# Three value-projection weight chunks loaded ahead of the second halves of x, and six row tiles in flight

## The chip, the cores and the metric

The kernel runs on one core of one Trainium2 chip. The metric is the device time of one execution in microseconds (us), given as the median of several runs of the same program. All work is in 32-bit floating point.

## What is computed

One layer of a decoder trunk over 1024 positions of width 1024: an RMS norm of `x`, one wide input projection, three branches (a spatial gate, a convolution, a cross-attention into 256 memory tokens), a gated merge, an output projection, a residual and a last norm. The change touches the start: the memory's keys and values, and the second 1024 columns of the input projection (`v`).

```python
h = rms_norm(x, norm_g[l])
z = jnp.einsum('bsd,de->bse', h, w_in[l])
v = layer_norm(jax.nn.gelu(z[..., OFF_A_V:OFF_A_V + W]), gmlp_ln_g[l], gmlp_ln_b[l])
...
mem_n = rms_norm(mem, mem_norm_g[l])
kv = jnp.einsum('bmd,de->bme', mem_n, w_kv)
...
proj = jnp.einsum('bsnw,nwd->bsnd', branches, w_branch[l])
merged = jnp.einsum('bsnd,bsnd->bsd', gates, proj)
x = x + jnp.einsum('bsd,de->bse', merged, w_out[l])
```

## The kernel before

**Products.** Every operand of a matmul is split into a high and a low part of a reduced-precision type: ScalarE casts the high part (L74), VectorE subtracts it from the source to get the low part (L75), and TensorE adds three products, high by high, low by high and high by low. A weight chunk is a tile of 128 partitions by 1024 elements (512 KB), loaded as `raw` (or `kraw`, `kvraw`) by SyncE and split into `whi` and `wlo`. The pool `raw` has three buffers, and the pool of `whi` and `wlo` has six, so three chunks of each are alive at once.

**Stages at the start.** First come the memory's keys (loop at L259, eight chunks `kraw`), then the memory's values (loop at L335, eight chunks `kvraw`, index `i` from 0 to 7), then the value projection of `x` (loop at L386). Its first pass (`th` = 0) covers the first 512 positions and takes eight weight chunks from `in_wv`, four for each half of the columns (`ch`). A chunk is 24 matmuls of 128x128 by 128x512 (L399). After the third chunk four more matmuls (L130) spread the row norms of `x` over all partitions into the tile `rb`. The second pass (`th` = 1) takes the same eight chunks for the other 512 positions. All later stages begin after that, at L445.

**Who loads what.** SyncE issues nearly all loads at the start, in the order of the program, from one queue. `xr` are the eight tiles of `x` turned round (128 channels by 1024 positions): their first halves (512 positions, 256 KB each) come during the keys and feed the first pass as `xg`; their second halves are issued at L360, all eight, at the end of the values' last chunk (`i` = 7). `xtok` are the eight row tiles of `x` (128 positions by 1024 channels, 512 KB each), used only for the sums of squares of the row norms (L135 to L138, on ScalarE for even and VectorE for odd tiles). `xt_load` loads one; `NXT` = 5 of them are started in chunks `i` = 2 to 6, and each call of `squares` that uses one up starts another, `NXT` further on. The first value-projection chunk is loaded where its loop comes to it:

```python
            if 2 <= i < 2 + NXT:
                xt_load(i - 2)
            if i in (5, 6):
                squares(1)
            if i == 7:
                for k in range(KT):
                    sload(xr[k][:, H:], xt[k][:, H:])
...
                hi, lo = wchunk(None, raw_load(wv[ch * 4 + c], True))
```

**What sets the order.** A scheduler orders the instructions of ScalarE, VectorE and TensorE; loads issued through `sload` or with `raw_load(..., True)` keep the program's order on SyncE. Each of SyncE's loads carries one of eight semaphores in turn and waits until the load eight places ahead of it has landed, so up to eight loads are in flight. GpSimd issues stores from a second queue, among them four of the keys (`kd`) and four of the values (`vd`, 512 KB each), after the values' results were taken out of PSUM (L365 on ScalarE, L366 on VectorE).

Of the kernel before, what the change touches and what calls it, by code (L numbers as in the profile page):

```python
# [19 lines left out]
KT = D // P  # L20
TT = S // P
H = 512
# [17 lines left out]
def trunk(ctx, tc, xt, x, memt, wf, wv, wkf, wkv, mem, wbr, wb1, wo, wst, bs, cols, fng, out):  # L40
# [13 lines left out]
    def nm(s):  # L54
        uid[0] += 1
        return f"{s}_{uid[0]}"

    def slot(dt=F32, shape=(P, 1024), s="s"):
        return slots.tile(list(shape), dt, tag="slot", name=nm(s))

    def op(shape=(P, 2, H), s="op"):
        return wpool.tile(list(shape), F32R, tag="op", name=nm(s), bufs=NOP)
# [4 lines left out]
    def bank(s="b"):  # L67
        return bank1.tile([P, H], F32, tag="b", name=nm(s))

    def f(ap):  # L70
        return ap.bitcast(F32)

    def split(src, hi, lo):
        A.copy(hi, src)  # L74
        V.tensor_tensor(lo, src, f(hi), ALU.subtract)  # L75

    def keep(ins):
        tc.keep_in_program_order(ins)

    def raw_load(src, pin=False):  # L80
        raw = wpool.tile([P, 1024], F32, tag="raw", name=nm("raw"), bufs=NRAW)
        ins = nc.sync.dma_start(out=raw, in_=src)
        if pin:
            keep(ins)
        return raw

    def wchunk(src, raw=None):
        hi, lo = op((P, 1024), "whi"), op((P, 1024), "wlo")
        split(raw_load(src) if raw is None else raw, hi, lo)
        return hi, lo  # L90
# [43 lines left out]
    def square(src, dst, vector=False):  # L134
        if vector:  # L135
            V.scalar_tensor_tensor(out=src, in0=src, scalar=1.0, in1=src, op0=ALU.mult, op1=ALU.mult, accum_out=dst)
        else:
            A.activation(out=src, in_=src, func=AF.Square, accum_out=dst)  # L138
# [9 lines left out]
    def store(dst, src):  # L148
        G.dma_start(out=dst, in_=src)
# [25 lines left out]
    xr = [None] * KT  # L175

    def sload(dst, src):
        keep(nc.sync.dma_start(out=dst, in_=src))
# [52 lines left out]
    def k_out(e, ps):  # L231
        hd, e2 = divmod(e, 2)
        if e2 == 0:
            kks[hd] = slot(F32R, (P, 2, 2, M), "k")
        kk = kks[hd]
        tmp = half("kt")
        V.tensor_tensor(tmp[:, :M], ps[:, :M], mrb, ALU.mult)
        split(tmp[:, :M], kk[:, 0, e2, :], kk[:, 1, e2, :])
        if e2 == 1:
            store(kdram[hd], f(kks.pop(hd)))  # L240
# [4 lines left out]
    def x_gain(k):  # L245
        v = xr[k][:, :H]
        xg[k] = slot(F32R, (P, 2, H), "xg")
        A.activation(out=xg[k][:, 0, :], in_=v, func=AF.Copy, scale=c1(COL_NORM, k))
        V.scalar_tensor_tensor(out=xg[k][:, 1, :], in0=v, scalar=c1(COL_NORM, k), in1=f(xg[k][:, 0, :]),
                               op0=ALU.mult, op1=ALU.subtract)  # L250
# [3 lines left out]
    def v_load(i):  # L254
        if i < KT:
            vraw[i] = slot(s="kvraw")
            sload(vraw[i], wkv[i])

    for g in range(2):  # L259
        pst = [bank() for _ in range(4)]  # L260
        for j in range(4):
            i = 4 * g + j
            if i == 0:
                hi, lo = op((P, 1024), "whi"), op((P, 1024), "wlo")
# [4 lines left out]
            elif g:  # L269
                hi, lo = wchunk(None, kraw[i])  # L270
            else:
                hi, lo = op((P, 1024), "whi"), op((P, 1024), "wlo")
# [4 lines left out]
            for kk2 in range(2):  # L277
                k = 2 * j + kk2
# [45 lines left out]
    def xt_load(t):  # L324
        xtok[t] = slot(s="xtok")
        sload(xtok[t], x[t * P:(t + 1) * P, :])

    def squares(n):
        for _ in range(n):
            t = min(xtok)  # L330
            square(xtok.pop(t), xss[:, t:t + 1], t % 2)
            if t + NXT < TT:
                xt_load(t + NXT)

    for hf in range(2):  # L335
        pst = [bank() for _ in range(MT)]
        for c in range(4):
            i = hf * 4 + c
            hi, lo = wchunk(None, vraw[i])
            v_load(i + 3)  # L340
            if i < 4:
                x_gain(4 + i)
            for m in range(MT):
                ms = slice(m * P, (m + 1) * P)
                for kk2 in range(2):
                    k = 2 * c + kk2
                    ws = slice(kk2 * H, (kk2 + 1) * H)
                    for j, (a, w) in enumerate(((mhi, hi), (mlo, hi), (mhi, lo))):
                        T.matmul(pst[m], a[k][:, ms], w[:, ws], start=(k == 0 and j == 0),
                                 stop=(k == KT - 1 and j == 2))  # L350
            if i < 2:
                for _ in range(2):
                    k_out(*late.pop(0))
            if 2 <= i < 2 + NXT:
                xt_load(i - 2)
            if i in (5, 6):
                squares(1)
            if i == 7:
                for k in range(KT):
                    sload(xr[k][:, H:], xt[k][:, H:])  # L360
        vv = [slot(F32R, (P, 2, MT, HD), "v") for _ in range(2)]
        for m in range(MT):
            for hh in range(2):
                hs = slice(hh * HD, (hh + 1) * HD)
                A.activation(out=vv[hh][:, 0, m, :], in_=pst[m][:, hs], func=AF.Copy, scale=mr[:, m:m + 1])  # L365
                V.scalar_tensor_tensor(out=vv[hh][:, 1, m, :], in0=pst[m][:, hs], scalar=mr[:, m:m + 1],  # L366
                                       in1=f(vv[hh][:, 0, m, :]), op0=ALU.mult, op1=ALU.subtract)
        for hh in range(2):
            store(vdram[hf * 2 + hh], f(vv[hh]))
# [16 lines left out]
    for th in range(2):  # L386
        va = [slot(s="va") for _ in range(4)]
        for ch in range(2):
            pst = [bank() for _ in range(4)]
            for c in range(4):  # L390
                hi, lo = wchunk(None, raw_load(wv[ch * 4 + c], True))
                for t in range(4):
                    ts_ = slice(t * P, (t + 1) * P)
                    for kk2 in range(2):
                        k = 2 * c + kk2
                        q = B[k // 4][1][k % 4] if th else xg[k]
                        ws = slice(kk2 * H, (kk2 + 1) * H)
                        for j, (a, w) in enumerate(((0, hi), (1, hi), (0, lo))):
                            T.matmul(pst[t], q[:, a, ts_], w[:, ws], start=(k == 0 and j == 0),  # L399
                                     stop=(k == KT - 1 and j == 2))  # L400
                i = ch * 4 + c
                if th == 0:
                    if i == 0:
                        squares(6)
                    elif i == 1:
                        xrs = mean_rsqrt(xss, TT, RMS_EPS)
                        xdg = diagonals(xrs, TT)
                    elif i == 2:
                        rb = slot(s="rb")
                        spread(xdg, rb, bank)  # L410
                    if i >= 2:
                        for _ in range(2 if i >= 6 else 1):
                            x_norm(nx, 1)
                            nx += 1
                elif i % 2 == 0:
                    x_norm(i // 2, 0)
                    x_norm(i // 2 + 4, 0)
                else:
                    combine(i // 2)
            for t in range(4):  # L420
                A.activation(out=va[t][:, ch * H:(ch + 1) * H], in_=pst[t], func=AF.Gelu_apprx_tanh,
                             scale=1.0 if th else xrs[:, t:t + 1])
        mv = small.tile([P, 4, 2], F32, tag="mv", name=nm("mv"))
        for t in range(4):
            st = small.tile([P, 2, 6], F32, tag="st", name=nm("st"))
            for hf in range(2):
                V.bn_stats(out=st[:, hf, :], in_=va[t][:, hf * H:(hf + 1) * H])
            V.bn_aggr(out=mv[:, t, :], in_=st)
        va_a = small.tile([P, 4], F32, tag="vaa", name=nm("va_a"))
        V.tensor_scalar(va_a, mv[:, :, 1], LN_EPS, None, ALU.add)  # L430
        vr = rsqrt(va_a, 4)
        vm = small.tile([P, 4], F32, tag="vam", name=nm("va_m"))
        V.scalar_tensor_tensor(out=vm, in0=mv[:, :, 0], scalar=-1.0, in1=vr, op0=ALU.mult, op1=ALU.mult)
        for t in range(4):
            A.activation(out=va[t], in_=va[t], func=AF.Identity, scale=vr[:, t:t + 1], bias=vm[:, t:t + 1])
            store(vadram[th * 4 + t], va[t])
# [741 lines left out]
PUMPA = 8  # L1178
NWARM = 10
NFILL = 7  # L1180
NXT = 5
PUMP = (6, 4, 6, 3, 6, 8, 6, 6, 5, 7)


# [55 lines left out]
```

## Time and profile before

| | us |
|---|---|
| median of 3 runs (1327.63 to 1329.01) | 1328.99 |
| profiled execution, its own time | 1329.95 |
| span of the profiled execution | 1328.2 |
| TensorE matmul busy | 1304.8 |
| VectorE busy | 1088.4 |
| ScalarE busy | 616.8 |

The profiled execution is 0.96 us above the median of the runs; its span, from the first to the last instruction, is 1.75 us shorter than its own time. TensorE's matmuls are recorded with modelled ends, so a busy TensorE says that it has work and not that it works at its peak; the granted clock says at which of its two rates it ran.

### The profile page before, as it was taken

Reading aid. Unit: us, or ns where it says so; the run is one execution under the profiler, and the core shown is the slowest. Engines: PE = TensorE matmul, PEld = TensorE weight load, DVE = VectorE, ACT = ScalarE, POOL = GpSimd, SP = SyncE. Lnnn points to the kernel's source line nnn. Section 1 sums busy time; section 2 is a strip of 40 time slices with the busy share of each in tenths; the row PEclk is TensorE's granted clock in tenths of the full one; section 3 lists DMA queues with packets and bytes.
Section 4 is the critical chain, followed back from the end, with each engine's and each line's share of the span. In section 5 each row is a group of like instructions: output and inputs, shape, how many; then the busy total and the mean of one; then the engine's idle time right before and its main releaser. Section 6 shows DMA issues by size and latency. Waiting matters only on the chain.

```text
span 1328.2 us, 16325 instructions
## 1 busy us (share of the span) xinstructions
PE 1304.8 (98%) x6010; PEld 1087.9 (82%) x6010; DVE 1088.4 (82%) x1468; ACT 616.8 (46%) x1012; POOL 114.7 (9%) x194
## 2 busy tenths in 40 slices
PE   9699999999999999999999999999999999999997
PEld 8588888888888888888888888888888888888886
DVE  6679859989968998986998996897589568895886
ACT  7546654445335345435435444445544543443245
POOL 0100000121000121100112100101000010000000
PEclk9899999999999999999999999999999999999999
DMA  9934333677524776534778526546644564555933
GB/s 331 411 115 146 104 112 120 212 241 232 169 80 143 233 209 214 193 95 115 221 236 247 156 85 168 175 153 223 242 155 163 173 224 141 207 207 208 406 130 127
DMA packets 82016, 249.74 MB, mean 188 GB/s; under 512 B 8336, under 2 KB 18064, under 8 KB 81936
## 3 DMA queue, kind: packets, MB, share of 16 engines
q1 hardware_dynamic: 55552, 153.44, 33.4%
q0 software_dynamic: 26096, 94.91, 23.0%
q8 instruction: 47, 0.77, 0.2%
q10 hardware_dynamic: 288, 0.35, 0.1%
q14 instruction: 33, 0.27, 0.1%
HBM read 176.84 MB, written 68.16 MB: 184 GB/s over the span
## 4 chain that ended last, share of the span: by engine, by line
PE 91%; DMA 5%; ACT 1%; DVE 1%; issue 1%; SPq 0%; POOL 0%; ACTq 0%; POOLq 0%
PE x L445 33%; PE y L445 16%; PE acc L775 12%; PE acc L976 10%; PE z L445 8%; PE b L399 7%; DMA xr<-in_xt 2%; PE acc L816 2%; PE acc L852 1%; PE sp L627 1%; DMA kvraw<-in_wkv 1%; DMA k<-kd 1%; DMA raw<-in_wv 1%; DMA mtok<-in_mem 1%; PE acc L837 0%
## 5 line engine op out<-in xcount | busy, mean ns | idle before, releaser
L445 PE MATMUL x<-T,op 128*128 128x512 f32 x1440 | 347.3, 390 | 0.0
L445 PEld LDWEIGHTS x<-T,op 128*128 128x128 f32 x1440 | 269.9, 188 | 56.4 <-ACT u L486 0.5
L74 ACT CAST op<-sum 128x512 fp32r<-128x512 f32 x160 | 99.4, 622 | 121.7 <-PE z L445 57.5
L550 DVE SCALAR_TENSOR_TENSOR conv<-cb,col,conv 128x994 f32<-128x994 f32 (+14 forms) x120 | 152.1, 1267 | 1.3 <-ACT conv L546 0.5
L75 DVE TENSOR_TENSOR op<-sum,op 128x512 fp32r<-128x512 f32 x160 | 110.0, 688 | 24.5 <-ACT op L74 24.3
L445 PE MATMUL x<-B,op 128*128 128x512 f32 x480 | 115.5, 389 | 0.0
L445 PE MATMUL z<-B,op 128*128 128x512 f32 x480 | 115.3, 389 | 0.0
L445 PE MATMUL y<-T,op 128*128 128x512 f32 x480 | 115.3, 389 | 0.0
L445 PE MATMUL y<-B,op 128*128 128x512 f32 x480 | 115.3, 389 | 0.0
L550 DVE SCALAR_TENSOR_TENSOR conv<-ca,col,conv 128x994 f32<-128x994 f32 (+14 forms) x90 | 114.0, 1267 | 0.4
L74 ACT CAST op<-raw 128x512 fp32r<-128x512 f32 x120 | 74.3, 620 | 73.2 <-PE y L445 71.8
L445 PEld LDWEIGHTS y<-B,op 128*128 128x128 f32 x480 | 90.1, 188 | 18.7
L445 PEld LDWEIGHTS x<-B,op 128*128 128x128 f32 x480 | 90.1, 188 | 18.7
L445 PEld LDWEIGHTS z<-B,op 128*128 128x128 f32 x480 | 90.1, 188 | 18.7
L445 PEld LDWEIGHTS y<-T,op 128*128 128x128 f32 x480 | 90.1, 188 | 18.7
L75 DVE TENSOR_TENSOR op<-raw,op 128x512 fp32r<-128x512 f32 x120 | 82.4, 687 | 24.4 <-ACT op L74 24.1
L775 PE MATMUL acc<-bhi,whi 128*128 128x512 f32 x256 | 79.7, 393 | 0.9 <-DVE ca L508 0.9
L775 PE MATMUL acc<-bhi,wlo 128*128 128x512 f32 x256 | 79.3, 390 | 0.0
L775 PE MATMUL acc<-blo,whi 128*128 128x512 f32 x256 | 79.2, 390 | 0.0
L976 PE MATMUL acc<-q,sw 128*128 128x512 f32 x288 | 65.4, 389 | 0.0
L976 PEld LDWEIGHTS acc<-q,sw 128*128 128x128 f32 x288 | 54.1, 188 | 11.2
L495 ACT COPY u<-x 128x512 f32<-128x512 f32 x40 | 23.5, 588 | 81.3 <-PE x L445 81.3
(267 smaller groups left out, 2169.1 us busy)
## 6 DMA issues: line engine op xcount, KB each, us to landing
raw<-in_wf SPq DMA_DIRECT2D x80, 512.0 KB, 3.7
sw<-sw SPq DMA_DIRECT2D x40, 512.0 KB, 7.8
sw<-wsh POOLq DMA_DIRECT2D x20, 512.0 KB, 4.3
sw<-ws POOLq DMA_DIRECT2D x20, 512.0 KB, 3.8
raw<-in_wv SPq DMA_DIRECT2D x16, 512.0 KB, 3.6
raw<-in_wbr SPq DMA_DIRECT2D x16, 512.0 KB, 5.4
gate<-g SPq DMA_DIRECT2D x16, 512.0 KB, 4.2
ws<-in_wb POOLq DMA_DIRECT2D x14, 512.0 KB, 6.5
```

Of the source, the lines that this page charges most:

```text
L74: A.copy(hi, src)
L75: V.tensor_tensor(lo, src, f(hi), ALU.subtract)
L399: T.matmul(pst[t], q[:, a, ts_], w[:, ws], start=(k == 0 and j == 0), stop=(k == KT - 1 and j == 2))
L445: T.matmul(ps, w[:, a, ks], m[k][:, b, :], start=(start and k == 0 and j == 0), stop=(stop and k == 3 and j == 2), skip_group_check=not start)
L495: A.copy(u3, x)
L550: V.scalar_tensor_tensor(out=a[:, PAD - j:], in0=g[:, :n], scalar=col[:, cw + j:cw + j + 1], in1=a[:, PAD - j:], op0=ALU.mult, op1=ALU.add)
L627: T.matmul(ps[:, t * P:(t + 1) * P], va[:, 4 * hf + t, :], ws[:, i, :], start=True, stop=True)
L775: T.matmul(ps[:, hf, :], w[:, ks], m[k][:, hf * H:(hf + 1) * H], start=(k == 0 and j == 0), stop=(k == KT - 1 and j == 2))
L816: T.matmul(ps[:, i, :], q[a][:, d, i * P:(i + 1) * P], kk[:, b, d, :], start=(d == 0 and j == 0), stop=(d == 1 and j == 2))
L852: T.matmul(ps[:, d, :], vv[:, a, m, d * P:(d + 1) * P], p2[b][:, m, :], start=(m == 0 and j == 0), stop=(m == MT - 1 and j == 2))
L976: T.matmul(ps[t], a[k][i][:, ts_], w[k][n], start=(start and k == 0 and j == 0), stop=(k == 3 and j == 2), skip_group_check=not start)
```

## The change

The loads of the first three weight chunks of the value projection are issued in the values' loop, one each at `i` = 5, 6 and 7, and handed on in a list. The second halves of `xr` are no longer issued at `i` = 7; four are issued in the value projection's first chunk and four in its second, after the chunk's weights are split in the code. `NXT` goes from 5 to 6.

```diff
+    wvraw = []
     for hf in range(2):
...
             if i in (5, 6):
                 squares(1)
-            if i == 7:
-                for k in range(KT):
-                    sload(xr[k][:, H:], xt[k][:, H:])
+            if i >= 5:
+                wvraw.append(raw_load(wv[i - 5], True))
...
-                hi, lo = wchunk(None, raw_load(wv[ch * 4 + c], True))
+                hi, lo = wchunk(None, wvraw.pop(0) if wvraw else raw_load(wv[ch * 4 + c], True))
+                if th == 0 and ch == 0 and c < 2:
+                    for k in range(4 * c, 4 * c + 4):
+                        sload(xr[k][:, H:], xt[k][:, H:])
...
-NXT = 5
+NXT = 6
```

On SyncE, at the end of the values' loop, the order is this (difference; `raw` are weight chunks of the value projection, `xtok` row tiles, `xr` second halves):

```order
 L178 DMA xtok_632<-in_x 128x1024
 L178 DMA xtok_635<-in_x 128x1024
-L178 DMA xtok_653<-in_x 128x1024
-L178 DMA xtok_656<-in_x 128x1024
+L82 DMA raw_637<-in_wv 128x1024
+L178 DMA xtok_655<-in_x 128x1024
+L178 DMA xtok_658<-in_x 128x1024
+L82 DMA raw_660<-in_wv 128x1024
+L178 DMA xtok_678<-in_x 128x1024
+L82 DMA raw_680<-in_wv 128x1024
 L178 DMA xr_240<-in_xt 128x512
 L178 DMA xr_242<-in_xt 128x512
```

The first weight chunk takes the place that the row tile `xtok_653` had, and the second and third stand among the row tiles. The eight second halves follow in both. Behind them, still on SyncE, the difference is this:

```order
 L178 DMA xr_375<-in_xt 128x512
 L178 DMA xr_414<-in_xt 128x512
-L82 DMA raw_703<-in_wv 128x1024
-L178 DMA xtok_734<-in_x 128x1024
-L82 DMA raw_741<-in_wv 128x1024
-L82 DMA raw_792<-in_wv 128x1024
 L82 DMA raw_835<-in_wv 128x1024
 L82 DMA raw_877<-in_wv 128x1024
```

What stands directly behind the second halves is now the fourth weight chunk (`raw_835`). On ScalarE, from the end of the values to the first weight splits of the value projection, it was before (`v` are the values taken out of PSUM, `whi` high parts):

```order
L138 ACTIVATE xtok_614,xss<-xtok_614 128x1024
L365 ACTIVATE v_682<-b_594,rs_y_287 128x256
L365 ACTIVATE v_682<-b_595,rs_y_287 128x256
L138 ACTIVATE xtok_653,xss<-xtok_653 128x1024
L365 ACTIVATE v_683<-b_594,rs_y_287 128x256
L365 ACTIVATE v_683<-b_595,rs_y_287 128x256
L138 ACTIVATE xtok_656,xss<-xtok_656 128x1024
L74 CAST whi_705<-raw_703 128x1024
```

and now it is:

```order
L138 ACTIVATE xtok_614,xss<-xtok_614 128x1024
L138 ACTIVATE xtok_635,xss<-xtok_635 128x1024
L74 CAST whi_703<-raw_637 128x1024
L138 ACTIVATE xtok_655,xss<-xtok_655 128x1024
L365 ACTIVATE v_682<-b_594,rs_y_287 128x256
L365 ACTIVATE v_682<-b_595,rs_y_287 128x256
L74 CAST whi_741<-raw_660 128x1024
L365 ACTIVATE v_683<-b_594,rs_y_287 128x256
L365 ACTIVATE v_683<-b_595,rs_y_287 128x256
L74 CAST whi_794<-raw_680 128x1024
```

The first weight cast stands ahead of the values' evictions, and the second and third stand between and behind them. VectorE follows the same pattern: the first weight subtraction stands ahead of the evictions, the second between them, and the last row tile's squares and the third subtraction stand directly ahead of the chain of the row norms (L109 to L121); in that chain itself stood, before, two weight subtractions. On TensorE the first six matmuls of the first chunk, and the first three of the second, now use only the high part of the weights; the rest stands as before.

## Rows read from the trace of the kernel before

**Rows 1.** The page's first section: busy us, share of the span, instructions.

```profile
PE 1304.8 (98%) x6010; PEld 1087.9 (82%) x6010; DVE 1088.4 (82%) x1468; ACT 616.8 (46%) x1012; POOL 114.7 (9%) x194
```

**Rows 2.** TensorE's waits, whole span: us in total, times, longest us.

```profile
PE b L399 <- ACT whi L74: 11.0, 1, 11.0
...
PE acc L775 <- DVE ca L508: 0.9, 1, 0.9
```

**Rows 3.** TensorE in order of time: values' end, first chunks, row norms' spread.

```profile
start us, us, engine line op out<-in xcount [idle before <-releaser]
54.54 0.39 PE L349 MATMUL b<-wlo,mhi 128*128 128x512 f32 x1
65.96 1.22 PE L399 MATMUL b<-whi,xg 128*128 128x512 f32 x2 [11.04 <-ACT whi L74]
...
74.42 0.62 PE L399 MATMUL b<-whi,xg 128*128 128x512 f32 x2
...
79.86 0.39 PE L399 MATMUL b<-whi,xg 128*128 128x512 f32 x1
...
85.30 1.09 PE L130 MATMUL b<-dg,onesr 128*128 128x512 f32 x4
86.23 0.62 PE L399 MATMUL b<-whi,xg 128*128 128x512 f32 x2
```

**Rows 4.** The split of the first chunk, and the chain's step into it.

```profile
56.69 8.10 DMA raw<-in_wv
...
64.86 1.04 ACT L74 CAST whi<-raw 128x1024 fp32r<-128x1024 f32 x1 [6.63 <-DMA raw<-in_wv]
```

**Rows 5.** SyncE's issues in order of time, each released by a landing eight places ahead.

```profile
37.31 0.33 SPq L178 DMA_DIRECT2D xtok<-in_x  x1
...
52.11 0.33 SPq L178 DMA_DIRECT2D xr<-in_xt  x1
54.58 0.33 SPq L178 DMA_DIRECT2D xr<-in_xt  x1
56.01 0.33 SPq L178 DMA_DIRECT2D xr<-in_xt  x1
```

**Rows 6.** Stretches: busy time by engine, granted clock of TensorE, DMA share, GB/s.

```profile
core 0: us, PE busy (x) PEld busy (x) DVE busy (x) ACT busy (x) POOL busy (x), PEclk, DMA share, GB/s
10.00:11.00 1.00, 0.49 (x4) 0.29 (x3) 1.00 (x3) 0.00 (x0) 0.00 (x0) 1.00 1.06 432
57.00:58.00 1.00, 0.00 (x0) 0.00 (x0) 0.74 (x2) 1.00 (x2) 0.00 (x0) 1.00 1.05 389
58.00:59.00 1.00, 0.00 (x0) 0.00 (x0) 0.00 (x0) 0.23 (x2) 0.53 (x1) 0.51 1.05 387
70.00:71.00 1.00, 1.00 (x4) 0.80 (x3) 0.93 (x4) 0.00 (x0) 0.00 (x0) 0.50 0.31 41
71.00:72.00 1.00, 1.00 (x4) 0.76 (x4) 0.87 (x3) 0.06 (x1) 0.00 (x0) 0.67 0.49 143
...
70.00:80.00 10.00, 10.00 (x42) 8.17 (x41) 5.60 (x12) 1.37 (x3) 0.00 (x0) 0.92 0.51 161
```

**Rows 7.** DMA from 28 to 34 us, and from 58 to 66 us by queue (q0 are GpSimd's stores).

```profile
DMA packets 774, 2.51 MB, mean 419 GB/s; under 512 B 87, under 2 KB 87, under 8 KB 773
...
q1 hardware_dynamic: 784, 2.27, 71.3%
q0 software_dynamic: 288, 1.05, 32.2%
```

**Rows 8.** VectorE's chain of the row norms, its first and last instruction.

```profile
68.34 0.17 DVE L109 TENSOR_SCALAR ms<-xss 128x8 f32<-128x8 f32 x1
...
74.06 0.68 DVE L121 TENSOR_TENSOR dg<-ident,rl 128x512 fp32r<-128x512 f32 x1
```

**Rows 9.** A later stretch, columns as in rows 6.

```profile
400.00:600.00 200.00, 200.00 (x900) 166.18 (x900) 179.16 (x225) 90.11 (x141) 25.32 (x40) 1.00 0.59 180
```

## Prediction

> **What bounds the kernel now.** I read the page's first section, then TensorE's waits, then TensorE, SyncE and ScalarE in order of time around the one long wait, then the stretches. TensorE is busy for 98% of the span [rows 1], and in its later stages it does not pause: 200.00 of 200 us from 400 to 600 us, beside 179.16 on VectorE [rows 9]. Its waits have one that counts: 11.0 us, once, at L399, for ScalarE's high part of a weight [rows 2]; the next one behind it is 0.9 us. So the time is TensorE's work plus its pauses, and this pause is nearly the whole of what can be had.
>
> The pause lies between the values' last matmul, which started at 54.54 us, and the value projection's first at 65.96 us [rows 3]. ScalarE had itself been idle for 6.63 us, and its cast began at 64.86 us, right after the weight chunk landed: issued at 56.69, plus 8.10 us, is 64.79 us [rows 4]. A chunk's landing is followed by TensorE's start 65.96 - 64.79 = 1.17 us later. The chunk was late because it stood behind other loads on a path that was full: the DMA share was 1.05 from 57 to 59 us [rows 6], and loads alone ran at 419 GB/s [rows 7].
>
> The pause also costs clock. TensorE stopped at about 54.9 us; from 57 to 58 us the granted clock was still 1.00 (2.4 GHz), from 58 us it was 0.50 (1.2 GHz), and it came back between 71 and 72 us, some 5 to 6 us after TensorE had resumed [rows 6]. The first chunk took 74.42 - 65.96 = 8.46 us, the second 79.86 - 74.42 = 5.44 us, each of 24 matmuls [rows 3]: 3.02 us for the half clock.
>
> **The first chunk's wait.** The moved chunk takes the place in SyncE's queue that a row tile of the same 512 KB had. That tile was issued at 37.31 us [rows 5]. Each load waits for the one eight places ahead, so the issue eight places behind tells its landing: 54.58 us [rows 5]. Nothing that stands ahead of this place is moved, its buffer was last read long before (the keys' splits), and the two stores of values issued by then are the same, so I put the chunk's landing at 54.56 us and TensorE's start at 54.56 + 1.17 = 55.73 us. On ScalarE the cast now has two squares ahead of it, one more than before; that one's row tile lands at 52.10 us (the issue at 52.11 [rows 5]) and ScalarE was idle there, so it is done before 53.3 us. Gain: 65.96 - 55.73 = 10.23 us. TensorE cannot start before about 54.8 us, so at most 0.9 us more could come.
>
> **The clock.** A pause of 0.8 to 1.0 us stays. In the rows the clock was still 1.00 some 3 us into a pause, and two pauses near 10 us (TensorE 0.49 busy in one microsecond) left it at 1.00 [rows 6]. So I take the half-clock stretch as gone: 3.02 us. The other end is that it stays, which costs the 3.02 us.
>
> **What the moved loads meet next.** Every load behind 54.56 us is later or earlier by what now stands ahead of it. A 512 KB load takes 56.01 - 54.58 = 1.43 us with the path to itself and 54.58 - 52.11 = 2.47 us beside a store [rows 5]. TensorE, at 5.44 us a chunk, wants the second chunk at 61.17 us, the third at 66.61, the spread of the norms at 72.05 and, 86.23 - 85.30 = 0.93 us later [rows 3], the fourth chunk at 72.98 us.
>
> The second chunk is three loads behind the first: 54.56 + 3 x 1.43 = 58.85 us. The values' stores cannot compete before that, since their evictions now stand behind the first cast and one more square. Its cast takes 1.04 us [rows 4] and its subtraction I estimate at the same or a little more, so the high part is there at 59.9 and the low part at about 61.2 us; the first three matmuls do without the low part. Margin about 1 us, cost nothing.
>
> The third chunk is two loads further: 61.7 us, or 63.8 us beside stores. Cast: 62.8 to 64.9 us. Margin 1.7 to 3.8 us.
>
> The norms' chain took from 68.34 to 74.74 us before [rows 8], with two weight subtractions inside it; it now follows the third chunk's subtraction (64.0 to 66.2 us by the casts above plus about 1.2). With the old length it ends at 70.4 to 72.6 us, without the two subtractions some 2 us earlier. Wanted at 72.05 us: cost nothing, at the worst 0.5 us.
>
> The fourth chunk is where the moved second halves of x press: ahead of it, from 54.56 us, stand five loads of 512 KB, eight of 256 KB and itself, 10 x 0.524 = 5.24 MB, and the two last stores of values, 1.05 MB [rows 7]. At 0.419 MB/us [rows 7] these 6.29 MB take 15.0 us: 69.6 us, cast done at 70.7 us, wanted at 72.98. Margin 2.3 us, cost nothing. The second halves themselves are in by then, and are first read after the spread at 72.98 us, so `rb` still comes last there. From the spread on, the queue has the same loads in the same order, the engines' orders differ in a few neighbouring rows, and everything moves ahead together. The sixth row tile in flight adds no bytes; it brings the last tile forward, to some 60.3 to 62.8 us, and that is what lets the norms' chain start by 66 us.
>
> A rule of the Trainium skill speaks against this step: "DMA: Bandwidth & Descriptors", section "Where 436 GB/s comes from", has loads from HBM bound at about 358 GB/s a core; by that figure the 6.29 MB would take 17.6 us, an estimate that puts the fourth chunk's cast at 73.2 us and costs 0.2 us (1315.9 us in the sum below). The trace, with 419 GB/s over 6 us [rows 7], decides for the faster rate.
>
> **The sum.** 10.23 + 3.02 = 13.25 us. Span 1328.2 - 13.25 = 1314.95 us; the profiled execution's own time 1329.95 - 13.25 = 1316.7 us. The median of the runs was 0.96 us below the profiled one, so I forecast 1328.99 - 13.25 = 1315.7 us.
>
> **Rivals.** First, the pause moves on: stores and loads share the path less well than in the sum, and TensorE waits for the second, third or fourth chunk or the spread, 1 to 4 us in all. For it: margins of 1 to 2.3 us behind one another. Against it: the rate of the path was steady at 387 to 432 GB/s in full stretches [rows 6]. Time: 1316.7 to 1319.7 us.
>
> Second, the change does not bring the chunk forward: the loads in flight share the path and one issued earlier lands no sooner. Up to seven loads issued before or with it would go first, 7 x 1.43 = 10.0 us, and the landing would be at 64.6 us again; the clock's loss stays, and the time is 1329 us. Against it: the issues at 52.11, 54.58 and 56.01 us, each released by one landing, come one load's length apart and in turn [rows 5]. "DMA: Bandwidth & Descriptors", section "Queues, rings and completion order", of the Trainium skill says that completion is not in order for one issuing engine; as far as these rows go, it was in order.
>
> Third, slower: the fourth chunk. It is issued only when the first of the second halves has landed, and stands behind 2 MB. It decides when its cast ends after 72.98 us; a pause of more than 3 us then also brings back the half clock, 3.02 us. To end above 1331.7 us (0.2% slower) the loss must be 15.9 us, so 12.9 us of pause, a landing at 84.7 us. From the late landing of the third chunk (63.8 us) there are 3.67 MB to move, so this needs 176 GB/s or less. From 70 to 80 us the rate was 161 GB/s [rows 6], but there the queue waited for buffers and the path was only half busy. At 161 GB/s: 22.8 us, landing at 86.6 us, 14.8 + 3.0 us lost, 1333.5 us.
>
> **How the numbers follow.** Forecast 0.77; the pause moves on 0.17; no gain 0.03; slower 0.02; a half-clock stretch that stays in spite of a short pause 0.01 (1318.7 us). A measurement of this kernel can tell about 0.2% (2.7 us) from no change. Faster: 0.77 + 0.17 + 0.01 = 0.95; same 0.03; slower 0.02. The range starts at 1315.7 less the 0.9 us that TensorE could still gain and half of the runs' spread of 1.4 us, rounded to 1314.0 us, and ends at the first rival's upper end, 1319.7 us.
>
> **What the profile will show.** TensorE's wait at L399 for ScalarE of 0.7 to 1.0 us in place of 11.0; its first value-projection matmul near 55.7 us; a granted clock of 1.00 in every stretch from 55 to 75 us; a first chunk of 5.4 us; the spread near 72.1 us; the fourth chunk's landing near 69.6 us with its cast before 73 us; no new wait above 1 us at L399 or L130; and the end of TensorE's work earlier by the same 13 us. A landing of the first chunk clearly behind 54.6 us, a granted clock below 1.00 before 75 us, or a second wait at L399 would make the prediction wrong, each by the amount above.

## The result, and the profile after

The changed kernel takes 1315.64 us (median of 4 runs, 1315.63 to 1316.36) against 1329.0 us for the kernel before (4 runs beside it, 1327.63 to 1331.53): a ratio of 0.9899, 95% interval 0.9881 to 0.9916, so 13.36 us less. The forecast was 1315.7 us. The profiled execution took 1315.63 us, with a span of 1313.9 us.

TensorE's waits in the changed kernel, whole span (us in total, times, longest us), answer to [rows 2]:

```profile
PE warm L206 <- POOL ones L161: 1.1, 1, 1.1
PE acc L778 <- DVE ca L511: 0.9, 1, 0.9
PE b L402 <- ACT whi L74: 0.6, 1, 0.6
```

The 11.0 us are gone from the head of the list; the same wait (the line is now L402) is third, with 0.6 us. TensorE in order of time answers to [rows 3]: the values' last matmul, the first of the value projection, the spread of the norms, the fourth chunk.

```profile
53.62 0.39 PE L350 MATMUL b<-wlo,mhi 128*128 128x512 f32 x1
54.60 1.66 PE L402 MATMUL b<-whi,xg 128*128 128x512 f32 x6 [0.59 <-ACT whi L74]
...
71.06 1.09 PE L130 MATMUL b<-dg,onesr 128*128 128x512 f32 x4
71.99 0.62 PE L402 MATMUL b<-whi,xg 128*128 128x512 f32 x2
```

From 54.60 to 71.06 us three chunks pass, 5.49 us each, where the first alone had taken 8.46 us. Behind the 0.59 us ahead of the first, no row of the three carries a wait. The chain of waits says what the start still hangs on (start, us, what):

```profile
36.27 17.14 DMA raw<-in_wv
54.60 16.61 PE b L402 x72
```

The first weight chunk lands at 53.41 us, and from 54.60 us TensorE runs 72 matmuls on end. ScalarE in order of time shows the four weight casts (of many rows):

```profile
53.51 1.05 ACT L74 CAST whi<-raw 128x1024 fp32r<-128x1024 f32 x1 [1.41 <-DMA raw<-in_wv]
...
57.63 1.05 ACT L74 CAST whi<-raw 128x1024 fp32r<-128x1024 f32 x1 [0.77 <-DVE xtok L136]
...
60.18 1.05 ACT L74 CAST whi<-raw 128x1024 fp32r<-128x1024 f32 x1 [0.77 <-DMA raw<-in_wv]
...
69.23 1.05 ACT L74 CAST whi<-raw 128x1024 fp32r<-128x1024 f32 x1 [4.63 <-DMA raw<-in_wv]
```

And the stretches, with columns as in [rows 6]:

```profile
56.00:60.00 4.00, 4.00 (x20) 3.29 (x19) 3.32 (x6) 2.65 (x7) 0.53 (x1) 1.00 1.03 397
60.00:64.00 4.00, 4.00 (x19) 3.33 (x18) 3.62 (x10) 1.26 (x2) 0.53 (x1) 1.00 1.06 399
64.00:68.00 4.00, 4.00 (x19) 3.30 (x18) 2.90 (x7) 0.20 (x1) 0.00 (x0) 1.00 1.03 413
68.00:72.00 4.00, 4.00 (x20) 3.28 (x19) 1.64 (x2) 2.38 (x3) 0.00 (x0) 1.00 0.49 200
```

TensorE is busy throughout, the granted clock stays at 1.00 (2.4 GHz), and the path of the loads is full until about 68 us.

**One sum for all executions.** The span can be cut in three: the start of the values' last matmul, the pauses in the value projection's first pass, and all the rest. This was done for every profiled execution of the study (us; the rest is the span less the other two):

| kernel | span | values' last matmul | pauses | rest |
|---|---|---|---|---|
| before | 1328.2 | 54.54 | 11.04 | 1262.6 |
| changed | 1313.9 | 53.62 | 0.59 | 1259.7 |
| changed, again | 1314.1 | 54.23 | 0.29 | 1259.6 |
| changed, third | 1315.0 | 54.75 | 0.44 | 1259.8 |
| first chunk alone | 1324.5 | 54.39 | 7.07 | 1263.0 |
| first chunk alone, again | 1327.6 | 56.29 | 8.28 | 1263.0 |
| halves moved alone | 1321.4 | 54.40 | 4.30 | 1262.7 |
| halves kept | 1314.3 | 54.05 | 0.47 | 1259.8 |
| five tiles | 1315.9 | 54.51 | 1.50 | 1259.9 |
| five tiles, again | 1314.4 | 53.56 | 1.50 | 1259.3 |
| five tiles, cast first | 1313.4 | 53.78 | 0 | 1259.6 |
| one step earlier | 1315.2 | 55.64 | 0 | 1259.6 |
| one load later | 1316.0 | 55.55 | 1.09 | 1259.4 |
| two megabytes more | 1321.2 | 53.88 | 5.01 | 1262.3 |

The rest has two levels and nothing between them: 1259.3 to 1259.9 us where no pause was above 1.5 us, and 1262.3 to 1263.0 us where one was 4.3 us or more. The 3 us between them are the half clock. So the 14.3 us between the two first spans are 10.45 us of pause, 2.9 us of clock and 0.92 us by which this execution's values happened to end earlier; the values' end differs by up to 2.7 us between executions. The medians, in which this largely evens out, differ by 13.36 us.

### The profile page after: what moved, and what is told of

Its sections match the earlier page's. It is cut to its first block, busy times and chain, and to the rows that moved or that the text cites. A ratio compares the mean times of both kernels' runs of the same rounds, so it can differ in the third digit from the quotient of the medians.

```text
span 1313.9 us, 16329 instructions
## 1 busy us (share of the span) xinstructions
PE 1301.2 (99%) x6010; PEld 1085.8 (83%) x6010; DVE 1088.4 (83%) x1468; ACT 616.9 (47%) x1012; POOL 115.5 (9%) x194
## 4 chain that ended last, share of the span: by engine, by line
PE 92%; DMA 4%; ACT 1%; DVE 1%; issue 1%; SPq 0%; POOL 0%; ACTq 0%; POOLq 0%
PE x L448 33%; PE y L448 17%; PE acc L778 12%; PE acc L979 10%; PE z L448 8%; PE b L402 7%; PE acc L819 2%; PE acc L855 1%; DMA raw<-in_wv 1%; PE sp L630 1%; DMA kvraw<-in_wkv 1%; DMA k<-kd 1%; PE acc L840 0%; ACT y L1124 0%; DMA mtok<-in_mem 0%
```

## The experiments

The theory: the gain is the first chunk's place in the queue (about 10 us of pause) and the half clock (about 3 us), and the other edits keep the pause from moving on. The kernels below undo or do one part each, or load one margin. Times are medians; each is set against the kernel before, or the changed one, on the same chip.

### The first chunk alone

```diff
+    wvraw = []
...
+            if i == 5:
+                wvraw.append(raw_load(wv[0], True))
             if i == 7:
...
-                hi, lo = wchunk(None, raw_load(wv[ch * 4 + c], True))
+                hi, lo = wchunk(None, wvraw.pop(0) if wvraw else raw_load(wv[ch * 4 + c], True))
```

> Only the first weight chunk is loaded ahead (at i = 5); the second and third are loaded where their loop comes to them, the second halves of x stay at i = 7, five row tiles in flight. Theory A (a queue in order at 419 GB/s, every chunk as late as the bytes ahead of it): the first matmul at L399 comes early, about 55.7 us, but the second chunk stands behind 4.2 MB of loads and 1.05 MB of stores and lands near 67 us where it is wanted at 61.2; TensorE waits some 7 us there, the clock halves for about 3 us of loss, and the whole gains about 3 us: 1325 to 1327 us. Rival (the first chunk's place alone carries the gain): no second wait, 1315 to 1317 us.

Measured: 1328.22 us (10 runs, 1325.01 to 1328.87), ratio 0.9993, interval 0.9984 to 1.0002: no gain that can be told, where theory A had expected about 3 us. The profiled execution took 1326.17 us, among the fastest of the ten. TensorE's rows in order of time:

```profile
54.39 0.39 PE L350 MATMUL b<-wlo,mhi 128*128 128x512 f32 x1
56.27 1.67 PE L402 MATMUL b<-whi,xg 128*128 128x512 f32 x6 [1.50 <-ACT whi L74]
67.61 1.22 PE L402 MATMUL b<-whi,xg 128*128 128x512 f32 x2 [5.57 <-ACT whi L74]
```

The first chunk starts 9.7 us earlier, and TensorE stops again after it, for 5.57 us. The issue of the second chunk's load, its time to landing, and ScalarE's rows show why:

```profile
57.45 0.41 SPq L82 DMA_DIRECT2D raw<-in_wv  x1
...
raw<-in_wv SPq DMA_DIRECT2D x1, 512.0 KB, 9.0
...
66.42 0.21 ACT L99 ACTIVATE rs_s<-ms 128x8 f32<-128x8 f32 x1 [7.38 <-DVE ms L109]
66.53 1.03 ACT L74 CAST whi<-raw 128x1024 fp32r<-128x1024 f32 x1
```

The second chunk stood in the queue behind the eight second halves and the last row tile. Issued at 57.45 us, it landed 9.0 us later, at about 66.45 us, and its cast began at 66.53 us. In ScalarE's order the cast also stands behind the norms' square root (L99), which waits for the last row tile; but that was done within 0.1 us of the landing, so the order cost almost nothing here. The pause moved on to the second chunk's landing, which theory A had put near 67 us. The clock fell all the same, and the rest is at its upper level.

The timed runs lay in two groups, near 1325 to 1326 and near 1328 to 1329 us. One more execution was to tell what lies between them.

> The kernel before with the first weight chunk alone loaded ahead, once more, since its timed runs lay in two groups, near 1325 to 1326 us and near 1328 to 1329 us, and the profiled one was of the lower. Theory A: whichever group this execution falls in, its span is the end of the values' matmuls plus the pauses at L402 plus about 1262.5 to 1263 us, so a time near 1328.5 us goes with pauses of about 9 us together in place of 7.1, or with a values' end about 2 us later. Rival B: the upper group has the same pauses and the same start, and the 2 to 3 us lie behind 80 us, or in a longer half-clock stretch.

Measured: one execution, 1329.33 us. TensorE's waits, then its two starts:

```profile
PE b L402 <- ACT whi L74: 8.3, 2, 6.8
PE b L282 <- ACT mhi L216: 2.2, 1, 2.2
```

```profile
56.29 0.39 PE L350 MATMUL b<-wlo,mhi 128*128 128x512 f32 x1
58.17 1.65 PE L402 MATMUL b<-whi,xg 128*128 128x512 f32 x6 [1.50 <-ACT whi L74]
70.69 1.22 PE L402 MATMUL b<-whi,xg 128*128 128x512 f32 x2 [6.78 <-ACT whi L74]
```

The rest is the same 1263.0 us. The 3.1 us more of span are 1.9 us of a later values' end and 1.2 us of a longer pause, as theory A had it, and both go with a queue of loads that ran later. The second chunk's load, its time to landing and its cast:

```profile
60.27 0.33 SPq L82 DMA_DIRECT2D raw<-in_wv  x1
...
raw<-in_wv SPq DMA_DIRECT2D x1, 512.0 KB, 8.9
...
69.61 1.03 ACT L74 CAST whi<-raw 128x1024 fp32r<-128x1024 f32 x1
```

The second chunk landed at about 69.2 us, 2.7 us later than in the other execution, while TensorE stopped 1.9 us later; that leaves 0.8 us of the longer pause. The other 0.4 us is ScalarE's order: here the square root came 0.3 us after the landing, and the cast behind it. The queue was late well before that: the first weight chunk was issued at 38.93 us, against 35.31 us. This explains these two executions; that all runs of the two groups differ so is likely and not shown.

### The second halves moved alone

```diff
-            if i == 7:
-                for k in range(KT):
-                    sload(xr[k][:, H:], xt[k][:, H:])
...
+                if th == 0 and ch == 0 and c < 2:
+                    for k in range(4 * c, 4 * c + 4):
+                        sload(xr[k][:, H:], xt[k][:, H:])
```

> Only the second halves of x are moved (four behind each of the first two weight chunks); no weight is loaded ahead, five row tiles in flight. Theory A: the first chunk stands behind two row tiles more than in the changed kernel and lands 2.9 us later; TensorE pauses 3.8 us at L399, which is longer than the 3.1 us after which the clock fell in the kernel before, so most of the half-clock loss of 3.0 us comes back; about 1321 to 1323 us, 1318.6 if the clock stays. Rival (loading weights ahead is what counts, moving x brings nothing): 1327 to 1329 us.

Measured: 1323.29 us (4 runs, 1321.79 to 1324.25), ratio 0.9958, interval 0.9941 to 0.9975. The wait at the first chunk is 4.30 us in place of 11.04, and the stretches show that the clock's loss stayed:

```profile
56.00:58.00 2.00, 0.00 (x0) 0.00 (x0) 0.88 (x2) 2.00 (x7) 0.62 (x2) 1.00 1.06 395
58.00:60.00 2.00, 0.91 (x2) 0.50 (x2) 0.93 (x1) 1.04 (x3) 0.44 (x1) 0.60 1.03 408
60.00:62.00 2.00, 1.96 (x5) 1.36 (x5) 1.04 (x2) 0.00 (x0) 0.00 (x0) 0.50 1.02 412
62.00:64.00 2.00, 2.00 (x6) 1.52 (x6) 1.54 (x8) 0.41 (x2) 0.00 (x0) 0.50 1.03 412
```

The first chunk's load, its time to landing and its cast, then the chain of waits, tell what is left of the pause:

```profile
41.47 0.33 SPq L82 DMA_DIRECT2D raw<-in_wv  x1
...
raw<-in_wv SPq DMA_DIRECT2D x1, 512.0 KB, 15.4
...
57.99 1.04 ACT L74 CAST whi<-raw 128x1024 fp32r<-128x1024 f32 x1
```

```profile
54.83 0.03 ACT v L363
...
55.20 0.68 ACT xtok L138
...
56.95 1.15 ACT xtok L138 x2
58.10 0.94 ACT whi L74
```

This edit alone is worth 4.9 us (by the two profiles 6.7 us of pause, with no clock won), because all eight halves go from ahead of the first weights. The chunk landed at 41.47 + 15.4 = 56.87 us, 2.1 us after TensorE had stopped. What holds the cast last is ScalarE's own order, evictions and two squares ahead of it: it began at 57.99 us, 1.1 us after the landing. So about 3.2 of the 4.3 us are the landing (an estimate: the landing plus the 1.1 us from the cast's start to TensorE's start in this run) and 1.1 us the order. A pause of 4.3 us lost as much clock as one of 11.

### Three chunks ahead, the second halves where they were

```diff
             if i >= 5:
                 wvraw.append(raw_load(wv[i - 5], True))
+            if i == 7:
+                for k in range(KT):
+                    sload(xr[k][:, H:], xt[k][:, H:])
...
-                if th == 0 and ch == 0 and c < 2:
-                    for k in range(4 * c, 4 * c + 4):
-                        sload(xr[k][:, H:], xt[k][:, H:])
```

> The changed kernel, but the second halves of x are issued at i = 7 as before, behind the third weight chunk's load. SyncE's order of loads comes out the same as in the changed kernel. Theory A (only the order in the queue counts): within 0.5 us of the changed kernel, 1315.1 to 1316.2 us. Rival (that the loads are issued later, inside the projection, counts): more than 1 us slower, 1317 us or above.

Measured: 1317.1 us (4 runs, 1315.98 to 1318.18), ratio 0.9912, interval 0.9897 to 0.9927. SyncE's loads stand in the same order as in the changed kernel, since in both the eight halves come behind the third weight chunk; the pause is 0.47 us and the rest 1259.8 us. With three chunks ahead, moving the halves in the code moves nothing in the queue. The median is 1.5 us above that of the changed kernel, which was not timed beside it, and 0.9 us above theory A's range; nothing in the profile answers to that, and the intervals overlap.

### Five row tiles in flight

```diff
-NXT = 6
+NXT = 5
```

> The changed kernel with five row tiles in flight instead of six. Theory A: the last row tile now stands among the second halves of x and lands near 65 us instead of 60; the chain of the row norms ends near 70.5 us against a spread wanted at 71.1 to 72 us, so nothing or less than 1 us is lost: 1315.5 to 1316.5 us. Rival (the sixth tile is needed to have the norms in time): TensorE waits 1 to 4 us before the spread at L130, 1317 to 1320 us.

Measured: 1317.66 us (4 runs, 1316.48 to 1318.44), ratio 0.9916, interval 0.9901 to 0.9931. The time is in the rival's range, but not by the rival's wait: the one at the first chunk is 1.50 us, and there is none at L130, where the prediction saw the sixth tile's use. On ScalarE, two evictions of values (L365) had come ahead of the first cast, and they wait for the values' last matmuls. To tell this from the norms, one kernel with five tiles has the first split written ahead of the evictions, and kept there:

```diff
+        if hf == 1:
+            first, src = (op((P, 1024), "whi"), op((P, 1024), "wlo")), wvraw.pop(0)
+            keep(A.copy(first[0], src))
+            keep(V.tensor_tensor(first[1], src, f(first[0]), ALU.subtract))
...
+                if hf:
+                    keep(ev)
+                    keep(el)
...
-NXT = 6
+NXT = 5
```

(`ev` and `el` are the two instructions that take out the values.) It ran beside the five tiles as they were and the changed kernel.

> The changed kernel with five row tiles in flight, as in the five-tile run, but with the first weight chunk's split written ahead of the values' evictions and kept there on ScalarE and VectorE. Its output is the same. Theory A (what five tiles cost was ScalarE's order: the cast stood behind two evictions, which wait for the values' last matmuls): ScalarE's cast begins when the chunk has landed, near 53.5 us, the pause at the first chunk falls from 1.5 us to 0.3 to 0.8 us, there is no wait at L130, and the time is that of the changed kernel, 1315.0 to 1316.5 us. Rival B (the sixth tile's place in the queue and the norms' chain, as the prediction's text had it): the pause shrinks, but a wait for the norms at L130 of about 1 us or more comes up, and the time stays near 1317.5 us. Rival C (the evictions held back behind the cast hold up the second chunk's cast): a wait of 0.5 to 2 us at the second chunk, 1316.5 to 1318 us.

> The changed kernel with five row tiles in flight, a second time, so that the run with the cast first is compared on the same chip. Theory A: ScalarE's cast behind two evictions, pause near 1.5 us at the first chunk, median 1317 to 1318 us, 1 to 2 us above the run with the cast first. Rival B: within 0.5 us of that run.

> The changed kernel as it is, beside the two with five tiles. All theories: 1315.0 to 1316.5 us, pause 0.3 to 1.0 us; theory A has the run with the cast first within 0.7 us of it, rival B about 2 us above it. Its start of the value projection and the values' end differ from execution to execution, so the pause and the end are read together: end between 53.6 and 55.6 us, time by about as much.

Measured, on one chip: five tiles with the cast first 1315.62 us (1315.13 to 1316.13), five tiles as they were 1316.95 us (1316.14 to 1317.43), the changed kernel 1315.5 us (1315.13 to 1316.74), 4 runs each. ScalarE with five tiles as they were:

```profile
52.63 0.47 ACT L365 ACTIVATE v<-b,rs_y 128x256 fp32r<-128x256 f32 x1 [3.93 <-PE b L350]
53.99 0.47 ACT L365 ACTIVATE v<-b,rs_y 128x256 fp32r<-128x256 f32 x1 [0.89 <-PE b L350]
54.36 1.03 ACT L74 CAST whi<-raw 128x1024 fp32r<-128x1024 f32 x1
```

and with the cast first:

```profile
52.79 1.05 ACT L363 CAST whi<-raw 128x1024 fp32r<-128x1024 f32 x1 [4.43 <-DMA raw<-in_wv]
53.74 0.47 ACT L369 ACTIVATE v<-b,rs_y 128x256 fp32r<-128x256 f32 x1
```

In the first the cast comes 0.8 us after the values' last matmul began (53.56 us), in the second 1.0 us before it (53.78 us), and TensorE goes from the values into the value projection without a recorded wait. The norms have time enough with five tiles: their chain was done 1.1 us ahead of the spread in both executions with five tiles as they were, and no wait is recorded at L130. Theory A holds for the time: the edit that changes only the order brings back 1.3 us by the medians, and leaves five tiles with the time of six. The pause at the first chunk shows it too. In all four executions in which the first cast stands behind two evictions (first chunk alone and five tiles, two each) it was 1.50 us, whether the chunk had landed 1.9 us before the values' last matmul began or 0.3 us after.

The profiled execution with the cast first had help besides: its chunk landed 1.1 us before the values' last matmul began, where it landed 0.2 to 0.3 us after in the two with five tiles as they were, and 0.2 to 0.5 us before with six tiles. At the landing of five tiles as they were, a cast put first would have left a pause of about 1.0 us (an estimate: the 1.50 us less the 0.5 us by which the cast began later behind the landing, 0.6 against 0.1 us). So the order is shown as the cause, and how much of the 1.3 us it is worth at one and the same landing is not.

### One step earlier, one load later

Loads of the three chunks at `i` = 4, 5 and 6:

```diff
-            if i >= 5:
-                wvraw.append(raw_load(wv[i - 5], True))
+            if 4 <= i < 7:
+                wvraw.append(raw_load(wv[i - 4], True))
```

> The changed kernel with the three weight loads issued one chunk earlier (at i = 4, 5 and 6). Theory A (the remaining pause is the first chunk's landing): the first chunk lands near 49 us, its cast is done before the values end, the pause of 0.6 to 0.8 us is gone, 0.5 to 0.8 us faster than the changed kernel run beside it. Rival (the remaining pause is a handover that no load removes, or row tiles pushed back cost as much): no difference, or slower.

The first chunk one load further back, behind the row tile that follows it:

```diff
+            if i == 6:
+                wvraw.append(raw_load(wv[0], True))
             if i in (5, 6):
                 squares(1)
-            if i >= 5:
+            if i >= 6:
                 wvraw.append(raw_load(wv[i - 5], True))
```

> The changed kernel with the first weight chunk one place later in the queue, behind one more row tile. It measures what a pause costs. Theory A (a load's length for a load's place; the clock falls only some 3 us into a pause): the pause becomes 2.0 to 2.4 us, the granted clock stays at 1.00, 1.3 to 1.6 us slower than the changed kernel. Rival (any pause above 1 us brings the half clock): 4 to 5 us slower.

Beside them, the changed kernel again:

> The changed kernel itself once more, beside the next three on the same chip. Theory A: 1315 to 1317.5 us, a pause of 0.5 to 1.0 us before the first matmul at L402, the granted clock at 1.00 through it. It also tells how far the start (the end of the values' matmuls, 53.6 us in the changed kernel's trace and 54.5 in that of the kernel before) moves between executions.

Measured, on one chip: changed 1315.72 us (4 runs, 1314.88 to 1316.99), one step earlier 1316.13 us (4 runs, 1314.68 to 1317.99), one load later 1318.18 us (5 runs, 1317.29 to 1320.0). One step earlier the first cast was at 51.03 us and the pause was gone:

```profile
55.64 0.39 PE L350 MATMUL b<-wlo,mhi 128*128 128x512 f32 x1
55.87 0.62 PE L402 MATMUL b<-whi,xg 128*128 128x512 f32 x2
```

That is worth at most the 0.3 to 0.6 us that the pause has in the changed kernel, which is less than these runs can tell: the median is 0.4 us the other way, and the values' end came late in the profiled execution (55.64 us). One load later, the chunk landed at about 55.8 us (issued at 38.72 us, 17.1 us to landing) and its cast began at 55.93 us. The pause is 1.09 us with the clock at 1.00 throughout. Theory A had 2.0 to 2.4 us: the chunk did land 2.1 us later than in the changed kernel beside it (53.7 us), but the values' end was late too, by 1.3 us (55.55 against 54.23 us). The two profiled executions are 1.9 us apart in span: 0.8 us of pause and 1.3 us of a later values' end, less 0.2 us in the rest.

The loads moved by the two edits did not cause the later ends. GpSimd's first store of keys tells it, first one load later, then in the changed kernel again:

```profile
33.13 0.68 POOL L149 DMA_DIRECT2D kd<-k  x1 [31.61 <-DVE k L75]
...
31.88 0.68 POOL L149 DMA_DIRECT2D kd<-k  x1 [30.36 <-DVE k L75]
```

The 1.3 us were there at 33.13 us, before the first load that differs was issued (35.59 us); one step earlier it was the same (33.29 us, and 34.57 us for the load). What is left open is why the medians of the two are 2.5 us apart, of which the profile shows 0.8 us as a pause.

### Two megabytes more ahead of the fourth chunk

The first halves of `xr`, already loaded, are loaded once more beside the second ones:

```diff
                         sload(xr[k][:, H:], xt[k][:, H:])
+                        sload(xr[k][:, :H], xt[k][:, :H])
```

> The changed kernel with the first halves of x loaded a second time beside each second half (the same bytes to the same place, nothing else changed): 2.1 MB or 5.0 us more ahead of the fourth weight chunk. It tests the margin of the fourth chunk. Theory A: the chunk lands near 74.2 us in place of 69.2, its cast ends near 75.3 to 76 where TensorE wants it at 72; a new wait of 3 to 4 us at L402, 3 to 4 us slower than the changed kernel, up to 7 if the clock falls as well. Rival (the second halves do not press on the weights): no new wait, within 1 us.

Measured: 1323.81 us (7 runs, 1322.86 to 1326.15), 8.1 us above the changed kernel on the same chip. TensorE in order of time, then the stretches:

```profile
75.88 1.65 PE L403 MATMUL b<-whi,xg 128*128 128x512 f32 x3 [4.28 <-ACT whi L74]
78.25 0.80 PE L403 MATMUL b<-wlo,xg 128*128 128x512 f32 x1 [0.73 <-DVE wlo L75]
```

```profile
72.00:74.00 2.00, 0.00 (x0) 0.00 (x0) 2.00 (x4) 0.96 (x3) 0.00 (x0) 1.00 1.03 408
74.00:76.00 2.00, 0.12 (x1) 0.12 (x1) 2.00 (x4) 1.64 (x3) 0.00 (x0) 0.64 0.68 268
76.00:78.00 2.00, 1.52 (x3) 0.70 (x3) 2.00 (x3) 1.80 (x2) 0.00 (x0) 0.50 0.04 14
78.00:80.00 2.00, 1.75 (x4) 1.46 (x5) 2.00 (x4) 1.50 (x2) 0.00 (x0) 0.50 0.42 45
```

The third rival's mechanism is real. The fourth chunk's cast began 6.05 us later after the first chunk's start than in the changed kernel (74.78 - 54.10 against 69.23 - 54.60), TensorE waited 5.0 us for its two parts, and the clock fell again, for 2.7 us more. The 3 to 4 us that theory A gave were too few, and so were the 7 us that it gave with the clock: the cast was a microsecond later than it had it (6.05 against 5.0 us), the clock was at 0.50 from 75 to 81 us, and the low part came later still, since its subtraction stood behind other work on VectorE (it began at 76.98 us, and TensorE had gone on with the high part at 75.88 us).

## Why the prediction was right, and where not

**What bounds the kernel** was right: with the one long wait gone, nothing took its place, and the time fell by that wait and its clock. That the median came within 0.1 us of the forecast is in part luck: the medians of the kernel before lay between 1327.96 and 1329.0 us in four sets of runs, and the two terms of the sum below were off by 0.2 and 0.1 us in opposite directions.

**The first chunk's wait** was right in size and cause: 10.45 us of pause went (11.04 to 0.59), 10.23 were forecast. The chunk landed 0.2 us before the last values' matmul began (53.41 and 53.62 us); forecast was 0.02 us after it (54.56 and 54.54). That the gain needs more than this load was only half seen: the first chunk alone, for which the sum would also give an early start, brought nothing that could be measured. What it needs is the second and third chunk's loads; with them, the halves left where they were in the code cost no pause (0.47 us).

**The clock** was right: 3.02 us forecast, 2.9 by the table, and 1.00 in every stretch of the changed kernel. Pauses of up to 1.5 us left it there.

**The second and third chunk** came sooner than forecast: casts at 57.63 and 60.18 us, where the landings alone had been put at 58.85 and 61.7 us or later. TensorE did not wait for either.

**The norms' chain** began and ended sooner than forecast. In the changed kernel VectorE begins it at 62.91 us, and its last product starts at 66.52 and takes 0.69 us: 4.3 us in all, where 6.4 stood in [rows 8] with the two subtractions inside. The "some 2 us" that the prediction gave for these were right. Its start had been put at 64.0 to 66.2 us, with the third chunk's subtraction, and that came sooner. It was done at 67.21 us, 3.9 us before the spread. The forecast had 70.4 to 72.6 us, or some 2 us less.

**The sixth row tile** is the step that failed. The prediction gave its use as the earlier last tile, "what lets the norms' chain start by 66 us". The tile does come earlier (issued at 45.96 us in the changed kernel, at 55.10 us with five tiles), but the norms had time in both; the 1.3 us between five tiles as they were and five with the cast first came from where the first cast stood on ScalarE. The new order was in the rows printed ahead of the prediction, and it got no price of its own: the prediction counted the squares ahead of the cast ("one more than before"), and not that the evictions, which wait for TensorE, had gone behind it.

**The fourth chunk** was right to within half a microsecond, by two errors that offset each other: the first chunk landed 1.15 us sooner than forecast, and the bytes behind it took 0.8 us longer (15.8 against 15.0 us). Its landing was forecast at 69.6 us, and its cast began on landing, at 69.23 us. The cast ended at 70.28 us and was wanted at 71.99 us: a margin of 1.7 us, forecast 2.3. From the first landing, 6.29 MB, loads and stores together, in 15.8 us are 398 GB/s. At the 358 GB/s that the Trainium skill gives for transfers to and from HBM ("DMA: Bandwidth & Descriptors", section "Where 436 GB/s comes from") they would have taken 17.6 us, an estimate; the measurement decides for the faster rate.

**The rivals.** The first, that the pause moves on, is what the first chunk alone did: TensorE waited for the second chunk, 5.6 to 6.8 us in place of the 1 to 4 us of the text. The second, no gain because transfers share, fell: the chunk issued earlier landed earlier, at 53.41 us. The third needs only some 2 us more ahead of the fourth chunk to begin, and did so under 2 MB more; the changed kernel stays clear of it by 1.7 us.

## What to carry to other kernels

A weight load moved ahead of bulk loads paid here only when the next ones were brought ahead with it, and 1.3 us more when its cast stood ahead of waiting work in the casting engine's order; check both before the queue's sum is believed. Where an engine's order and a landing come close together, check when the load landed before the order is blamed. Pauses of TensorE of 4.3 us and more cost the pause plus some 3 us of clock here, pauses of 1.5 us or less no more than themselves; what lies between was not measured. Cut spans into start, pauses and rest: that told a half-microsecond pause from a 2 us drift of the start, which the medians of four runs could not.

## What the runs showed of the hardware

In the five executions with a pause of 4.3 us or more (the longest 11.0 us), the granted clock was 1.00 (2.4 GHz) while TensorE worked and into the pause. It fell to 0.50 (1.2 GHz) when TensorE had been still for 3.0 to 4.2 us, and was 1.00 again 5.4 to 6.5 us after it had resumed (read from stretches of half a microsecond). So the loss was nearly the same, 2.7 to 3.4 us, whatever the pause. In the nine executions with pauses of 1.5 us or less the clock was 1.00 in every stretch from 53 to 85 us.

The values' last matmul began anywhere from 53.56 to 56.29 us. In all fourteen executions it began 22.3 to 22.4 us after GpSimd's first store of keys (31.21 to 33.95 us), so the whole difference lies in what comes ahead of that store. In the latest execution 2.2 us of it were one wait at L282 for the memory's high parts (1.0 us in the other execution of that kernel); the cause of the rest is open.
